# Matmul with batch normalisation: x and w loaded as bf16 by casting DMAs, and a streamed operand with a step of two

## The chip, the cores and the metric

One core of a Trainium2 chip. The metric is the device time of one execution in microseconds (us), the median of several. A profile shows one execution; its span is about 1.8 us shorter than the time. Runs are sorted into fast and slow by time and by the granted TensorE clock. The profile of the kernel before (span 296.1) fell on a run marked slow, a little above the median of its fast ones.

## The reference

```python
batch, m, k, n = 16, 512, 1024, 768
y = np.matmul(x, weight)                       # x: 16 x 512 x 1024, weight: 1024 x 768, fp32
mean = np.mean(y, axis=(0, 1), keepdims=True)  # per column, over all 8192 rows
var  = np.var(y, axis=(0, 1), keepdims=True)
out  = gamma * (y - mean) / np.sqrt(var + eps) + beta
```

The statistics of a column need all 8192 rows, so nothing can be stored before all of x has been multiplied by that column's weights.

## The kernel before

x comes in tiles of 256 rows (1 MB of fp32, `q` = 0 to 31). Each tile is brought in by four DMAs: quarter `i` of the columns goes to partitions 32i to 32i+31. GpSimd casts a tile to bf16, putting two rows side by side in a 4-byte word; VectorE transposes 32x32 blocks of such words; TensorE multiplies. A unit of work, called a *matmul tile* here, is 8 matmuls of 128x512: one of 6 column tiles (`nt`) times one of 16 chunks of 512 rows (`c`). Before the statistics of the first three column tiles (`GA = 3`) are complete, 63 of the 96 matmul tiles are done: all six column tiles for the first five chunks, three for the other eleven.

```python
def load_x(q):
    x_st = stage.tile([P, QT, KQ], f32, tag="st")          # three buffers
    rows = x_flat[q * QR:(q + 1) * QR].rearrange("(t r) k -> r t k", r=32)
    for i in range(4):
        eng = nc.sync if i < 2 else nc.scalar
        seq(eng.dma_start(x_st[32 * i:32 * i + 32], rows[:, :, KQ * i:KQ * (i + 1)]))

def cast_x(q, part):                                        # GpSimd, two parts of a tile
    x_bf = xbpool.tile([P, UP, KQ, 2], bf16, tag="xb")
    ...
def turn_x(q, part):                                        # VectorE
    ...
    seq(nc.vector.transpose(dst[:, half, part * UP:(part + 1) * UP], src))

def mm(nt, c):
    for jj in range(KT):
        seq(nc.tensor.matmul(y_ps, w_sb[:, jj, nt * P:(nt + 1) * P], xT[c][:, jj, :], ...))
def bn(nt, c):   seq(nc.vector.bn_stats(stats[:, nt, c, :], py[nt, c]))
def keep(nt, c): seq(nc.scalar.copy(y_sb, py.pop((nt, c))))
...
# all of these are put in order by a planned time: at(t, fn, ...)
at(t, load_affine)        # the 12 small gamma and beta DMAs, on GpSimd
```

The order on each engine is fixed by planned times, so a VectorE statistic can stand behind a transpose whose load is late.

## Time and profile before

| | before |
|---|---|
| time, median (range) | 296.28 us (295.21 to 297.46) |
| last transpose of x ends (the last load lands at 162.2) | 172.1 us |
| T1: statistics of the first three column tiles complete, aggregation starts | 193.3 us |
| T1 to the end | 102.8 us |
| mean rate over the span, HBM | 209 GB/s |

T1 is where the first bn aggregate starts in the chain of work. Everything before it is loading and multiplying; everything after is the output stage. The rows behind this table are in the prediction.

### The profile page before, as it was taken

How to read it: one execution, taken by the hardware profiler on the slowest of the kernel's cores; microseconds unless marked ns; L12 is line 12 of the kernel's file. 1: busy time of each engine (PE TensorE's matmuls, PEld its weight loads, DVE VectorE, ACT ScalarE, POOL GpSimd, SP SyncE). 2: the span in 40 equal slices, each digit the busy share in tenths (PEclk: the TensorE clock that was granted, in tenths of full speed). 3: DMA queues.
4: the chain of work that ended last, by engine and by line, in shares of the span. 5: the costliest groups of instructions: out<-in, count | busy, mean ns of one | idle time of the engine just before them, and what ended most of it. 6: DMA issues, size and time to landing. Idle time of an engine off the chain costs nothing.

```text
span 296.1 us, 3319 instructions
## 1 busy us (share of the span) xinstructions
PE 210.9 (71%) x1132; PEld 102.7 (35%) x1152; DVE 149.6 (51%) x285; ACT 99.4 (34%) x154; POOL 89.3 (30%) x83
## 2 busy tenths in 40 slices
PE   0019996597097875695647659989897999997630
PEld 0003442233043332232213224446564555554530
DVE  0344653626435554545452173387766656656751
ACT  2001221112122212121102033339796866566230
POOL 0333545436636565564642940000000000000000
PEclk9999999879779999797887959999999999999655
DMA  7999999999999999999999000007999797666997
GB/s 175 304 232 297 208 251 264 220 209 211 206 203 213 235 220 225 231 220 221 223 231 170 3 1 2 0 0 265 360 357 363 259 278 217 178 197 179 281 265 215
DMA packets 71889, 62.10 MB, mean 210 GB/s; under 512 B 3264, under 2 KB 71872, under 8 KB 71872
## 3 DMA queue, kind: packets, MB, share of 16 engines
q1 hardware_dynamic: 52448, 43.52, 57.3%
q10 hardware_dynamic: 19040, 18.35, 30.4%
q8 instruction: 9, 0.15, 0.2%
q0 software_dynamic: 384, 0.01, 0.1%
q14 instruction: 8, 0.07, 0.1%
HBM read 36.71 MB, written 25.17 MB: 209 GB/s over the span
## 4 chain that ended last, share of the span: by engine, by line
DMA 56%; PE 26%; DVE 6%; POOL 5%; ACT 4%; issue 2%; ACTq 0%; SPq 0%; DVEq 0%; POOLq 0%
DMA x_st<-in_x_dram 46%; PE y_ps L156 23%; DMA out_dram<-o_sb 8%; PE o_ps L193 3%; ACT o_sb L201 3%; POOL x_bf L136 3%; DMA w_st<-in_weight_dram 2%; DVE y_sb L180 2%; DVE stats L162 1%; POOL beta_sb L106 1%; POOL gamma_sb L105 1%; DVE o_sb L203 1%; ACT y_sb L167 1%; DVE mv L172 0%; DVE xT_sb L150 0%
## 5 line engine op out<-in xcount | busy, mean ns | idle before, releaser
L156 PE MATMUL y_ps<-xT_sb,w_sb 128*128 128x512 bf16 x748 | 187.9, 403 | 65.5 <-ACT y_sb L167 43.3
L156 PEld LDWEIGHTS <-w_sb 128*128 128x128 bf16 x768 | 77.6, 103 | 164.2 <-issue 82.5
L167 ACT CAST y_sb<-y_ps 128x512 bf16<-128x512 f32 x96 | 56.0, 588 | 163.4 <-DMA x_st<-in_x_dram 92.6
L136 POOL CAST x_bf<-x_st 128x1024 bf16<-128x1024 f32 x64 | 82.1, 1328 | 84.0 <-DMA x_st<-in_x_dram 81.8
L150 DVE STREAM_TRANSPOSE xT_sb<-x_bf 128x512 f32<-128x512 f32 x64 | 45.4, 711 | 82.0 <-POOL x_bf L136 82.0
L162 DVE BATCH_NORM_STATS2 stats<-y_ps 128x6 f32<-128x512 f32 x96 | 65.0, 678 | 36.5 <-PE y_ps L156 36.2
L201 ACT CAST o_sb<-o_ps 128x768 f32<-128x768 bf16 (+1 forms) x52 | 44.9, 886 | 24.5 <-DMA out_dram<-o_sb 13.0
L193 PE MATMUL o_ps<-ident,y_sb 128*128 128x128 bf16 x384 | 31.2, 231 | 9.8 <-DVE y_sb L180 6.9
L180 DVE TENSOR_SCALAR y_sb<-y_sb,scale,shift 128x512 bf16<-128x512 bf16 x96 | 33.2, 404 | 0.0
L193 PEld LDWEIGHTS <-y_sb 128*128 128x128 bf16 x384 | 26.2, 104 | 19.1 <-DVE y_sb L180 9.3
L122 DVE CAST w_sb<-w_st 128x2048 bf16<-128x2048 f32 x3 | 3.7, 1228 | 12.1 <-DMA w_st<-in_weight_dram 12.1
L203 DVE CAST o_sb<-o_ps 128x1024 f32<-128x1024 bf16 x4 | 4.9, 1225 | 6.1 <-DMA out_dram<-o_sb 5.2
L105 POOL DMA_DIRECT2D gamma_sb<-in_gamma_dram x6 | 3.4, 559 | 0.0
L106 POOL DMA_DIRECT2D beta_sb<-in_beta_dram x6 | 3.2, 536 | 0.0
L172 DVE BATCH_NORM_AGGREGATE mv<-stats 128x2 f32<-128x96 f32 x6 | 3.2, 561 | 0.0
L174 DVE RECIPROCAL scale<-std 128x1 f32<-128x1 f32 (+1 forms) x4 | 0.7, 167 | 3.9 <-ACT std L173 3.9
L97 ACT ACT_TABLE_LOAD x1 | 1.3, 1283 | 0.7 <-PEq L301 0.7
L173 ACT ACTIVATE std<-mv,eps_sb 128x1 f32<-128x1 f32 (+1 forms) x4 | 1.2, 304 | 0.8 <-DVE mv L172 0.8
L176 DVE TENSOR_TENSOR tmp<-mv,scale 128x1 f32<-128x1 f32 (+1 forms) x4 | 0.6, 160 | 0.1
L177 DVE TENSOR_TENSOR shift<-beta_sb,tmp 128x1 f32<-128x1 f32 (+1 forms) x4 | 0.6, 160 | 0.1
L175 DVE TENSOR_TENSOR scale<-scale,gamma_sb 128x1 f32<-128x1 f32 (+1 forms) x4 | 0.6, 159 | 0.1
masks.py:199 POOL TENSOR_SCALAR_AFFINE_SELECT ident<-ident 128x128 bf16<-128x128 bf16 x1 | 0.3, 288 | 0.0
(7 smaller groups left out, 0.9 us busy)
## 6 DMA issues: line engine op xcount, KB each, us to landing
x_st<-in_x_dram SPq DMA_DIRECT2D x64, 256.0 KB, 8.5
x_st<-in_x_dram ACTq DMA_DIRECT2D x64, 256.0 KB, 8.7
out_dram<-o_sb SPq DMA_DIRECT2D x16, 768.0 KB, 4.7
out_dram<-o_sb SPq DMA_DIRECT2D x24, 512.0 KB, 3.6
w_st<-in_weight_dram SPq DMA_DIRECT2D x6, 256.0 KB, 6.8
w_st<-in_weight_dram ACTq DMA_DIRECT2D x6, 256.0 KB, 6.7
gamma_sb<-in_gamma_dram POOLq DMA_DIRECT2D x6, 0.5 KB, 2.2
beta_sb<-in_beta_dram POOLq DMA_DIRECT2D x6, 0.5 KB, 2.3
```

What stands on the lines that cost most here:

```text
L105: seq(nc.gpsimd.dma_start(gamma_sb[:, nt:nt + 1], gamma[nt * P:(nt + 1) * P, None]))
L106: seq(nc.gpsimd.dma_start(beta_sb[:, nt:nt + 1], beta[nt * P:(nt + 1) * P, None]))
L122: seq(nc.vector.tensor_copy(w_sb[:, :, n0:n0 + WN], wst.pop(part)))
L136: seq(copy(x_bf.rearrange("p u k h -> p h u k"), xs[q].rearrange("p (h u) k -> p h u k", h=2)[:, :, part * UP:(part + 1) * UP, :],))
L150: seq(nc.vector.transpose(dst[:, half, part * UP:(part + 1) * UP], src))
L156: seq(nc.tensor.matmul(y_ps, w_sb[:, jj, nt * P:(nt + 1) * P], xT[c][:, jj, :], start=(jj == 0), stop=(jj == KT - 1),))
L162: seq(nc.vector.bn_stats(stats[:, nt, c, :], py[nt, c]))
L167: seq(nc.scalar.copy(y_sb, py.pop((nt, c))))
L180: seq(nc.vector.tensor_scalar(y[nt, c], y[nt, c], scale[:, nt:nt + 1], shift[:, nt:nt + 1], op0=ALU.mult, op1=ALU.add,))
L193: seq(nc.tensor.transpose(o_ps[:, s, a, :], cols, ident))
L201: seq(nc.scalar.copy(ost[key][:, part], src))
L203: seq(nc.vector.tensor_copy(ost[key][:, part], src))
```

## The change

x and w are brought in by GpSimd DMAs that cast on the way, so the GpSimd casts of x and the VectorE casts of w go, and half as many bytes reach SBUF. A 4-byte word then holds two neighbouring columns of one row, not two rows. After the transpose the even and the odd columns lie interleaved, so a matmul reads its streamed operand with a step of two, and w is laid out to match. Three smaller things go with it: four buffers for a tile of x in place of three, w in two parts in place of three, and the 12 gamma and beta DMAs now stand behind all loads on GpSimd. The diff is abridged.

```diff
+    XB = 4
-        x_st = stage.tile([P, QT, KQ], f32, tag="st")
+        x_bf = xbpool.tile([P, QT, KQ], bf16, tag="xb")
         rows = x_flat[q * QR:(q + 1) * QR].rearrange("(t r) k -> r t k", r=32)
         for i in range(4):
-            eng = nc.sync if i < 2 else nc.scalar
-            seq(eng.dma_start(x_st[32 * i:32 * i + 32], rows[:, :, KQ * i:KQ * (i + 1)]))
-    def cast_x(q, part): ...
+            seq(nc.gpsimd.dma_start(x_bf[32 * i:32 * i + 32], rows[:, :, KQ * i:KQ * (i + 1)]))
 ...
-            eng = nc.sync if i < 2 else nc.scalar
-            seq(eng.dma_start(w_st[32 * i:32 * i + 32], ...))
-    def cast_w(part): ...
+            for e in range(2):
+                seq(nc.gpsimd.dma_start(w_sb[32 * i:32 * i + 32, :, e, n0:n1], rows[i, e, :, :, n0:n1]))
 ...
-        for jj in range(KT):
-            seq(nc.tensor.matmul(y_ps, w_sb[:, jj, nt * P:(nt + 1) * P], xT[c][:, jj, :], ...))
+        for jw in range(JW):
+            for e in range(2):
+                seq(nc.tensor.matmul(y_ps, w_sb[:, jw, e, nt * P:(nt + 1) * P], xT[c][:, jw, :, e], ...))
 ...
-                cols = y[nt, c][:, half * QR:(half + 1) * QR].rearrange("p (m h) -> p h m", h=2)[:, h]
-                seq(nc.tensor.transpose(o_ps[:, s, a, :], cols, ident))
+                seq(nc.tensor.transpose(o_ps[:, s, a, :], y[nt, c][:, i * P:(i + 1) * P], ident))
```

## The prediction

> **What bounds the kernel now.** I read the page's chain of work first, then the chain in order of time, then the queue view in two narrow windows, then the costly groups.
>
> The chain that ended last, by line:
>
> ```profile
> DMA 56%; PE 26%; DVE 6%; POOL 5%; ACT 4%; issue 2%; ACTq 0%; SPq 0%; DVEq 0%; POOLq 0%
> DMA x_st<-in_x_dram 46%; PE y_ps L156 23%; DMA out_dram<-o_sb 8%; PE o_ps L193 3%; ACT o_sb L201 3%; POOL x_bf L136 3%; DMA w_st<-in_weight_dram 2%; DVE y_sb L180 2%; DVE stats L162 1%; POOL beta_sb L106 1%; POOL gamma_sb L105 1%; DVE o_sb
> ```
>
> Loading x alone is 46% of the span. The chain in order of time shows where that stretch ends (start, length, what):
>
> ```profile
> 158.16 4.03 DMA x_st<-in_x_dram
> ...
> 162.29 1.33 POOL x_bf L136
> 163.62 0.59 POOL gamma_sb L105
> ...
> 169.48 0.53 POOL beta_sb L106
> 170.00 1.34 POOL x_bf L136
> 171.36 0.71 DVE xT_sb L150
> ...
> 173.33 7.33 PE y_ps L156 x25
> 180.71 10.74 PE y_ps L156 x49
> ...
> 193.27 1.39 DVE mv L172 x3
> ```
>
> So there are three stages: loading, until the last transpose of x ends at 172.1 us; a remainder of matmuls (78 of them), until the statistics of the first three column tiles are complete at 193.3 (call this T1); and the output stage, from T1 to 296.1, which is 102.8 us. In the last, TensorE is busy nearly throughout until 272, and then stores drain. The 12 small gamma and beta DMAs put 6.4 us into the path between the last two casts.
>
> Why does loading take so long? 35.65 MB in some 160 us is 220 GB/s with the DMA engines never idle. Two windows of 1 us in the queue view, first at 12 us and then at 19 us:
>
> ```profile
> DMA packets 358, 0.35 MB, mean 345 GB/s; under 512 B 21, under 2 KB 358, under 8 KB 358
> ## 3 DMA queue, kind: packets, MB, share of 16 engines
> q10 hardware_dynamic: 181, 0.17, 56.0%
> q1 hardware_dynamic: 177, 0.17, 54.5%
> ```
>
> ```profile
> DMA packets 235, 0.23 MB, mean 229 GB/s; under 512 B 11, under 2 KB 235, under 8 KB 235
> ## 3 DMA queue, kind: packets, MB, share of 16 engines
> q10 hardware_dynamic: 200, 0.20, 97.6%
> q1 hardware_dynamic: 35, 0.03, 16.2%
> ```
>
> When both queues move equally, 345 GB/s; when one queue does nearly all, 229. SyncE's queue (q1) loads partitions 0 to 63, ScalarE's (q10) partitions 64 to 127, each DMA to 32 partitions. So I read the slow rate as the SBUF side: one half of the partitions takes about 220 GB/s.
>
> **What the Trainium skill says.**
> 1. "SBUF — State Buffer", section "Door 1: The DMA port swizzle": partitions 0 to 31, and 0 to 63, reach 8 of the 16 ports, 64 to 127 the other 8; the limit for eight ports is about 218 GB/s. The trace agrees (229 with a little from the other half, 345 with both).
> 2. "DMA: Bandwidth & Descriptors", section "SWDGE vs HWDGE vs iDMA": a DMA that casts must be issued by GpSimd, whose cores write the descriptors in software. In the trace a GpSimd DMA of 128 descriptors takes 0.53 us of the engine (the beta rows). Nothing in the trace shows one of 256.
> 3. "SBUF — State Buffer", the note on cachelines: lines of 16 bytes, two hits per line are enough for full speed. A step of two in bf16 makes four. The trace has a case on the weight side: y_sb is read with a step of two, w_sb densely, and the loads take 104 and 103 ns. For the streamed operand nothing shows it.
> 4. Same page, "Who interferes with whom": two-port VectorE copies hold GpSimd off from writing descriptors. The only such copies in the loading stage are the three casts of w, and they go.
>
> The groups that the change touches:
>
> ```profile
> L156 PE MATMUL y_ps<-xT_sb,w_sb 128*128 128x512 bf16 x748 | 187.9, 403 | 65.5 <-ACT y_sb L167 43.3
> L136 POOL CAST x_bf<-x_st 128x1024 bf16<-128x1024 f32 x64 | 82.1, 1328 | 84.0 <-DMA x_st<-in_x_dram 81.8
> L150 DVE STREAM_TRANSPOSE xT_sb<-x_bf 128x512 f32<-128x512 f32 x64 | 45.4, 711 | 82.0 <-POOL x_bf L136 82.0
> L162 DVE BATCH_NORM_STATS2 stats<-y_ps 128x6 f32<-128x512 f32 x96 | 65.0, 678 | 36.5 <-PE y_ps L156 36.2
> L106 POOL DMA_DIRECT2D beta_sb<-in_beta_dram x6 | 3.2, 536 | 0.0
> ```
>
> GpSimd, VectorE and TensorE all wait for the loads here, directly or by one step.
>
> **The change part by part.**
> - *Removed:* 64 casts on GpSimd (82.1 us) and 3 on VectorE (3.7 us). They lay beside the loads, save two casts' latency of 1.33 us per tile of x in how early a transpose and so a refill can start. ScalarE no longer issues loads, so its copies out of PSUM no longer queue behind a load's wait (TensorE lost 43.3 us to those copies). The gamma and beta DMAs now come after all loads on GpSimd: 6.4 us off the path.
> - *Moved:* the same 35.65 MB are read from HBM, but 128 + 16 DMAs now come from one GpSimd queue, and half the bytes are written into SBUF. In one queue the quarters of x come one after another, so mostly one half of the ports is in use. If that half takes 220 GB/s of bf16, it no longer limits: that would be 440 GB/s of fp32 read. I then take the best rate that loads of 1 KB pieces reach in this trace, 340 to 345 GB/s: 0.77 us per DMA of 256 KB, 3.1 us per MB.
> - *GpSimd's cost:* if 0.53 us were all per descriptor, 256 would take 1.06 us; if all fixed, 0.53. I take 0.7 to 0.8, so about level with the transfer. The program's order also shows eight completion semaphores in rotation: each DMA waits for the one eight before it, so 2 MB are in flight. At 340 GB/s that is 6.2 us, above the 2.2 us that a small GpSimd DMA takes to land, so the queue stays fed.
> - *Transposes:* 32 of 128x1024 words in place of 64 of 128x512. From 0.711 us for 512 and an estimated one word per cycle of 0.96 GHz (533 ns, so 178 fixed): 1.25 us each, 40 us in place of 45.4. No gain by itself.
> - *TensorE:* same 768 matmuls of 0.216 us (8 in 1.73 us in the chain); I assume that the step of two costs nothing.
>
> *The sum.* Start: 8 weight DMAs (1 MB), two tiles of x, then 2 MB of weights, 5 MB in all: at about 0.55 us each for the smaller ones and 0.75 for x, GpSimd has issued these by 16 us; the weights have landed at about 20. Then 30 tiles of x: 30 x 3.1 = 92 us, so the last lands at 112 and is transposed at 114. The order on VectorE fixes what follows: 15 statistics stand behind the last transpose (13 before). TensorE can be some 3 tiles ahead: before, 78 matmuls, or 9.75 tiles of 8, remained, and took 21.2 us. Now 11.75 remain: 20.3 us, plus about 1.7 for a cold start and the last statistics, so T1 = 136. The output stage has the same instructions in the same order on VectorE and SyncE: 102.8 us. End: 136 + 103 = 239; I say 240.
>
> The floor if loads were infinitely fast: TensorE has 63 tiles x 1.73 = 109 us before T1, two of them before 20 us: T1 = 20 + 105.5 + 1 = 126.5, end 229.
>
> **The rivals.**
> (a) *Descriptor writing becomes the bound.* At 1.0 us per DMA of x: 20 + 120 + 2 + 22 = 164, end 267. For it: GpSimd does all loads alone, and 0.53 us for 128 has an unknown split. Against: an instruction has a fixed part.
> (b) *The casting transfer is slow, or a single load queue is,* so that some 220 GB/s of fp32 stay the limit: 30 x 4.77 = 143, T1 = 187, end 290, nearly nothing gained but the gamma loads. For it: no single-queue load above 240 GB/s is in this trace. Against: a single queue stores at 360 GB/s (mean of 207 to 230 us), so an engine can do it.
> (c) *The step of two halves the matmul rate.* 768 x 0.43 = 330 us of matmuls: far slower, near 400. For it: nothing measured on the streamed side. Against: the weight side shows no cost.
> (d) *Loads are faster than 345 GB/s:* then TensorE bounds, 229 to 233.
>
> **Range and chances.** I weigh the main case and (d) at 55%, (a) or something halfway to it at 27%, (b) at 11%, (c) or another loss at 7%. The range 228 to 280 holds the main case and most of (a). Faster by over 2% means under 290.2: 0.87; within 2%: 0.06; slower: 0.07.
>
> **What would show it.** Right: the load rate near 340 GB/s until about 112 us, GpSimd's DMA instructions at 0.7 to 0.8 us, transposes at 1.25 us, matmul spacing 0.216 us, T1 near 136, and 103 us from there to the end. (a) shows as GpSimd issuing back to back at about 1 us with idle DMA engines; (b) as DMA engines fully busy at 220 GB/s; (c) as 8 matmuls in well over 1.73 us in the output stage. What makes it wrong most likely is the load rate, to which the end follows one for one: each 0.1 us per DMA of x is 12 us.

## The result, and the profile after

| | before | after | predicted |
|---|---|---|---|
| time, median (range) | 296.28 (295.21 to 297.46) | 243.24 (242.32 to 244.05) | 240 |
| last transpose of x ends | 172.1 | 109.0 | 114 |
| first matmul | 20.9 | 17.2 | two tiles before 20 |
| T1 | 193.3 | 134.8 | 136 |
| T1 to the end of the span | 102.8 | 106.8 | 103 |

The ratio is 0.821 (95% interval 0.817 to 0.825). A ratio is the mean time of one kernel's fast runs over that of the other's fast runs of the same rounds, so it is not quite the ratio of the medians quoted. All four runs of the kernel before on this chip count as fast, at 295 to 297 us. On two other chips, where its fast runs were at 289 to 293, the same step gave 0.835 (0.830 to 0.840, run c1) and, with an order that changed nothing, 0.837 (0.827 to 0.847, run e6). So the gain is 16 to 18%.

The chain of work that ended last, by engine and by line, for the kernel after:

```profile
PE 70%; DMA 15%; ACT 5%; DVE 4%; POOL 2%; issue 2%; ACTq 0%; POOLq 0%; DVEq 0%
```

The DMA's 56% have become 15%, most of it the stores at the end; TensorE's 26% have become 70%. In order of time (start, length, what), the whole loading stage is now one row of matmuls:

```profile
12.34 4.85 DMA w_sb<-in_weight_dram
17.19 11.40 PE y_ps L138 x40
...
29.23 1.24 DVE xT_sb L131
...
30.52 103.54 PE y_ps L138 x456
...
134.08 0.70 DVE stats L144
134.78 1.39 DVE mv L154 x3
```

456 matmuls in 103.54 us are 0.227 us each, where the prediction counted 0.216. The wait before 17.19 is put down to a weight load, but the second transpose of x also ends only at 17.1 (it starts at 15.89 and takes 1.25), so the start waits for both. VectorE's own order after the last transpose (start, length, engine, and in brackets the idle time before) shows the same from the other side:

```profile
107.76 1.25 DVE L131 STREAM_TRANSPOSE xT_sb<-x_bf 128x1024 f32<-128x1024 f32 x1 [0.18 <-DMA gamma_sb<-in_gamma_dram]
108.93 0.66 DVE L144 BATCH_NORM_STATS2 stats<-y_ps 128x6 f32<-128x512 f32 x1
110.51 0.70 DVE L144 BATCH_NORM_STATS2 stats<-y_ps 128x6 f32<-128x512 f32 x1 [0.92 <-PE y_ps L138]
112.33 0.70 DVE L144 BATCH_NORM_STATS2 stats<-y_ps 128x6 f32<-128x512 f32 x1 [1.11 <-PE y_ps L138]
```

From 110 us on every statistic waits for its matmuls, 1.81 us apart, and 14 of them follow. The groups of the changed lines (busy us, mean ns, then idle before):

```profile
L138 PE MATMUL y_ps<-xT_sb,w_sb 128*128 128x512 bf16 x768 | 182.2, 393 | 17.3 <-DMA w_sb<-in_weight_dram 17.2
...
L120 POOL DMA_DIRECT2D x_bf<-in_x_dram x128 | 73.1, 576 | 17.9 <-issue 6.6 <-DMA x_bf<-in_x_dram 4.6 <-DVE stats L144 2.5
...
L131 DVE STREAM_TRANSPOSE xT_sb<-x_bf 128x1024 f32<-128x1024 f32 x32 | 39.4, 1231 | 17.0 <-DMA x_bf<-in_x_dram 16.8
...
L111 POOL DMA_DIRECT2D w_sb<-in_weight_dram x16 | 8.8, 554 | 1.9 <-DMA x_bf<-in_x_dram 0.8
```

GpSimd spends 0.576 us on a DMA of 256 pieces, and 0.542 us (median) on one of 128 pieces: nearly all of it is fixed. The idle time before these matmuls fell from 65.5 to 17.3 us, 17.2 of it before the first one. (A piece is an unbroken run of the source in the program, 1 KB for x; the number of descriptors is not in the trace.) In the queue view of the kernel after, 17 of the 40 slices of the window 30 to 110 us read 190 to 194 GB/s, at a mean of 174; DMA bytes are counted as written here, at half size, so 193 is 386 GB/s of fp32 read: the steady best, and not the mean. Over the stage, 120 DMAs were issued from 16.7 to 103.1 us, 0.72 us each.

In the output stage one group of 8 matmuls took 3.28 us, and the granted clock there was half (two rows of the chain, then the window with its clock in the third place from the end):

```profile
172.02 3.28 PE y_ps L138 x8
...
176.11 1.80 PE y_ps L138 x8
172.00:175.40 3.40, 3.40 (x12) 1.30 (x10) 1.84 (x7) 1.29 (x2) 0.00 (x0) 0.51 0.69 249
```

### The profile page after: what moved, and what is told of

Its sections match the earlier page's. It is cut to its first block, busy times and chain, and to the rows that moved or that the text cites. A ratio compares the mean times of both kernels' runs of the same rounds, so it can differ in the third digit from the quotient of the medians.

```text
span 241.6 us, 3150 instructions
## 1 busy us (share of the span) xinstructions
PE 204.7 (85%) x1152; PEld 98.9 (41%) x1152; DVE 143.6 (59%) x250; ACT 100.1 (41%) x154; POOL 89.2 (37%) x163
## 4 chain that ended last, share of the span: by engine, by line
PE 70%; DMA 15%; ACT 5%; DVE 4%; POOL 2%; issue 2%; ACTq 0%; POOLq 0%; DVEq 0%
PE y_ps L138 65%; DMA out_dram<-o_sb 11%; PE o_ps L173 4%; ACT o_sb L181 4%; POOL w_sb L111 2%; DMA w_sb<-in_weight_dram 2%; DMA x_bf<-in_x_dram 2%; DVE y_sb L162 1%; DVE stats L144 1%; DVE mv L154 1%; ACT y_sb L149 1%; DVE xT_sb L131 1%; DVE o_sb L183 1%; ACT std L155 0%; DVE scale L156 0%
## 5 line engine op out<-in xcount | busy, mean ns | idle before, releaser
L138 PE MATMUL y_ps<-xT_sb,w_sb 128*128 128x512 bf16 x768 | 182.2, 393 | 17.3 <-DMA w_sb<-in_weight_dram 17.2
L138 PEld LDWEIGHTS <-w_sb 128*128 128x128 bf16 x768 | 73.4, 97 | 113.2 <-issue 12.2
L144 DVE BATCH_NORM_STATS2 stats<-y_ps 128x6 f32<-128x512 f32 x96 | 66.8, 696 | 64.6 <-PE y_ps L138 64.6
L120 POOL DMA_DIRECT2D x_bf<-in_x_dram x128 | 73.1, 576 | 17.9 <-issue 6.6
L131 DVE STREAM_TRANSPOSE xT_sb<-x_bf 128x1024 f32<-128x1024 f32 x32 | 39.4, 1231 | 17.0 <-DMA x_bf<-in_x_dram 16.8
L111 POOL DMA_DIRECT2D w_sb<-in_weight_dram x16 | 8.8, 554 | 1.9 <-DMA x_bf<-in_x_dram 0.8
```

The costliest lines, as they stand in the source:

```text
L111: seq(nc.gpsimd.dma_start(w_sb[32 * i:32 * i + 32, :, e, n0:n1], rows[i, e, :, :, n0:n1],))
L120: seq(nc.gpsimd.dma_start(x_bf[32 * i:32 * i + 32], rows[:, :, KQ * i:KQ * (i + 1)]))
L131: seq(nc.vector.transpose(dst[:, half], src))
L138: seq(nc.tensor.matmul(y_ps, w_sb[:, jw, e, nt * P:(nt + 1) * P], xT[c][:, jw, :, e], start=(jw == 0 and e == 0), stop=(jw == JW - 1 and e ...
```

## The experiments

The theory after the result: the loads of the kernel before were held by the side of SBUF that they write, because each DMA goes to partitions of one half (0 to 63 or 64 to 127); halving the bytes lifts that limit; then TensorE sets the pace, slowed a little by the step of two. The rivals: the gain came from leaving the two hardware queues (with ScalarE's issue standing between its copies) or from dropping the casts; the longer spacing of matmuls came from TensorE running without gaps; the loads still set the pace. A further one, the fourth buffer of x, falls with e2, which has four buffers too.

Runs e1, e2, e3, e5 and e7 give wrong results.

### e2: the same DMAs without the cast

```diff
-        x_bf = xbpool.tile([P, QT, KQ], bf16, tag="xb")
+        x_bf = stage.tile([P, QT, KQ], f32, tag="st")            # STAGE = 4
-        src = xs.pop(q).rearrange("p t k -> p (t k)").bitcast(f32)
+        src = xs.pop(q).rearrange("p t k -> p (t k)")[:, :QT * KQ // 2]
-                    ... xT[c][:, jw, :, e],
+                    ... xT[c][:, jw, :, 1],
```

The transposes and matmuls are as many and as large as in the changed kernel. Only the loads of x write 256 KB in place of 128 KB.

> The changed kernel with x brought in as fp32 by the same GpSimd DMAs, no cast, full-size writes (wrong result: the upper halves are multiplied for even and odd columns alike). If halving the bytes written to one half of the ports is what made loading fast: about 220 to 230 GB/s of x, 1.14 to 1.2 us per DMA, the last x landing near 160 us, T1 near 183 us and the end near 290 us. If the gain came from leaving the SyncE and ScalarE queues and dropping the GpSimd casts: 0.72 us per DMA as in the changed kernel and 243 us.

Measured: 303.79 us median (301.08 to 308.08), T1 at 200.2. The window 40 to 90 us of its queue view:

```profile
DMA packets 3124, 10.25 MB, mean 205 GB/s; under 512 B 626, under 2 KB 626, under 8 KB 3122
```

The whole gain is gone, although all other parts of the change are in place. The rival of the queues and the casts falls. The rate was lower than I had expected (205, not 220 to 230) because the 229 of the kernel before had some traffic to the other half in it: from 60 to 61 us, where q10 moved 10 of 212 packets, that kernel reads 203. And e2 is slower than the kernel before, whose two queues overlapped for part of the time (222 GB/s from 30 to 160 us).

### e3: full-size writes, but across all partitions

```diff
 # on top of e2
-        rows = x_flat[q * QR:(q + 1) * QR].rearrange("(t r) k -> r t k", r=32)
+        rows = x_flat[q * QR:(q + 1) * QR].rearrange("(t r) k -> r t k", r=P)
-            seq(nc.gpsimd.dma_start(x_bf[32 * i:32 * i + 32], rows[:, :, KQ * i:KQ * (i + 1)]))
+            seq(nc.gpsimd.dma_start(x_bf[:, 2 * i:2 * i + 2], rows[:, :, KQ * i:KQ * (i + 1)]))
```

> As e2_fp32_32, but each of the four DMAs of a tile spans 128 partitions with the same 256 pieces of 1 KB (wrong result: rows lie where columns should). If it is the half of the ports that limits full-size writes: 340 GB/s or more, at most 0.77 us per DMA, T1 at 135 to 140 us, end 243 to 248 us. If it is the bytes written as such, or the single queue: as slow as e2_fp32_32, near 290 us.

Measured: 242.57 us (241.53 to 242.82), T1 at 138.2. The same window:

```profile
DMA packets 5124, 16.82 MB, mean 336 GB/s; under 512 B 1024, under 2 KB 1024, under 8 KB 5121
```

Same bytes, same queue, no cast, and packets of 4 KB in both runs (the queue view has the pieces of 1 KB put together): 336 GB/s in place of 205. So it is not the number of bytes written that counts but how many partitions share them. One thing else differs in e3, and in e5 below: a DMA reads its rows in another order, and no run changes that order alone. In e3 GpSimd needs 0.714 us per DMA and is the pace of the loads.

### e5: the kernel before, with loads across all partitions

```diff
-        rows = x_flat[q * QR:(q + 1) * QR].rearrange("(t r) k -> r t k", r=32)
+        rows = x_flat[q * QR:(q + 1) * QR].rearrange("(t r) k -> r t k", r=P)
-            seq(eng.dma_start(x_st[32 * i:32 * i + 32], rows[:, :, KQ * i:KQ * (i + 1)]))
+            seq(eng.dma_start(x_st[:, 2 * i:2 * i + 2], rows[:, :, KQ * i:KQ * (i + 1)]))
```

> The kernel before, only each load of x spanning 128 partitions (wrong result). If half of the ports limits its loads: x at 340 GB/s or more, the last transpose near 115 us, T1 near 137 us, end near 240 us, with the GpSimd casts still in place. If the alternation of the two queues or the casts are the limit: 296 us unchanged.

Measured: 248.16 us (246.18 to 248.75), T1 at 143.9. The window 40 to 90 us:

```profile
DMA packets 17977, 17.39 MB, mean 348 GB/s; under 512 B 1057, under 2 KB 17971, under 8 KB 17971
## 3 DMA queue, kind: packets, MB, share of 16 engines
q1 hardware_dynamic: 8987, 8.67, 54.5%
q10 hardware_dynamic: 8984, 8.66, 53.7%
```

The kernel before, with its GpSimd casts and its two queues, comes within 5 us of the changed one as soon as its loads spread over all partitions. It is 8 us above what I expected: the last transpose ended at 124.5 us and not near 115, and VectorE waited 29.4 us for the GpSimd casts. This cannot be used as it stands: the quarters of the columns have to lie in different groups of 32 partitions for the block transpose, and these loads put them elsewhere.

### e8: the kernel before, each queue alternating between the halves

```diff
-        for i in range(4):
-            eng = nc.sync if i < 2 else nc.scalar
+        for i in (0, 3, 2, 1):
+            eng = nc.sync if i % 2 == 0 else nc.scalar
```

> The kernel before, each queue alternating between the halves of the partitions: SyncE loads quarters 0 and 2, ScalarE quarters 3 and 1 (correct). If the halves are the limit and each queue alone now reaches both: over 260 GB/s on average in the loading stage and 260 to 280 us. If one queue works one DMA at a time: the two queues can still meet in the same half, some 230 GB/s, 285 to 296 us.

Measured: 304.85 us (302.17 to 307.03), ratio 1.045 (1.034 to 1.057); correct. It is slower, and by more than the range of either branch. One microsecond of its queue view, at 60 us:

```profile
DMA packets 202, 0.20 MB, mean 204 GB/s; under 512 B 3, under 2 KB 202, under 8 KB 202
## 3 DMA queue, kind: packets, MB, share of 16 engines
q10 hardware_dynamic: 103, 0.10, 56.9%
q1 hardware_dynamic: 99, 0.10, 56.4%
```

Here both queues move equally and the rate is still 204. Equal queues alone are therefore not what makes loads fast. The profile doesn't list the partition of a packet, but the trace has each packet's queue, start and size, and a DMA of x is 256 packets. Counting them off in the order of issue puts SyncE on quarter 2 and ScalarE on quarter 3 in this microsecond: the same half. Over 5 to 160 us, half a microsecond after a slice of 0.1 us in which one half of the partitions got 90% of the bytes or more, the median rate was 202 GB/s (933 slices); after one in which both halves got about the same, it was 259 (179 slices). The rate 0.6 us later correlates with the balance of the halves at 0.64, and with the balance of the queues at 0.25. So e8 fits the halves; it lost because its queues met in one half most of the time.

The same question has to be put to the kernel before. In some of its microseconds the queues moved almost equally and slowly: from 16 to 17 us, 132 packets of q1 and 103 of q10, at 225 GB/s. In windows of 0.2 us, 16.0 to 16.2 and 16.8 to 17.0, they turn out to take turns:

```profile
q1 hardware_dynamic: 50, 0.05, 103.3%
q10 hardware_dynamic: 5, 0.01, 9.8%
...
q10 hardware_dynamic: 41, 0.04, 109.1%
q1 hardware_dynamic: 2, 0.00, 1.5%
```

Side by side for several microseconds they reached 335 GB/s (9 to 13 us) and 342 (22 to 26). From 30 to 160 us they mostly took turns, and the mean was 222. Why they fell into taking turns is open.

### e6 and e7: alternating the halves within GpSimd's single queue

```diff
 # e6: on the changed kernel; e7: on e2
-        for i in range(4):
+        for i in (0, 2, 1, 3):
```

> The changed kernel with the four DMAs of a tile of x in the order of quarters 0, 2, 1, 3, so that neighbours in the queue go to opposite halves of the ports (correct). If half of the ports still limits the casting loads (193 GB/s written against 206 in e2_fp32_32) and neighbours overlap: more than 193 GB/s written; the end gains at most 1 to 2 us, since TensorE sets most of the pace. If GpSimd's pace, buffers or the read side limit: unchanged, 243 us.

> e2_fp32_32 (full-size writes, wrong result) with the quarters in the order 0, 2, 1, 3. If it is the half of the ports and neighbours in one queue overlap: well over 206 GB/s and an end under 285 us. If the engines work one DMA at a time, so that the halves take turns anyway: 206 GB/s and 303 us unchanged.

Measured: e6 243.39 us (241.92 to 245.24), correct, unchanged, and its best slices read the same 190 to 194 GB/s. e7 288.68 us (286.58 to 290.93), 231 GB/s in the window where e2 had 205. So neighbours in one queue do overlap a little, which helps full-size writes by 13% in rate. That falls between my two branches. Casting loads get nothing from it; what holds them at 386 GB/s of fp32 stays open.

### e1: the step of two taken away

```diff
-                    ... xT[c][:, jw, :, e],
+                    ... xT[c].rearrange("p jw m e -> p (jw m e)")[:, (2 * jw + e) * CH:(2 * jw + e + 1) * CH],
```

> The changed kernel with the streamed operand read densely (wrong result: the words stay interleaved). If the step of two is what stretches a matmul from 0.216 to 0.227 us and TensorE sets the pace of the loading stage too: 8 matmuls back to 1.73 us, T1 (the first bn aggregate) at 134.8 - 63 x 8 x 0.0106 = 129.5 us, and the end 768 x 0.0106 = 8 us earlier, 235 us. If the longer spacing comes of TensorE running without gaps (power or clock), nothing changes: 1.81 us and 243 us. If the loads set the pace of the loading stage, T1 stays at 134.8 and only the output stage gains 3 us.

Measured: 236.41 us (235.41 to 238.24), T1 at 131.0. Two rows of its chain, one before T1 and one after:

```profile
118.99 10.74 PE y_ps L138 x49
...
140.77 1.73 PE y_ps L138 x8
```

Eight matmuls take 1.73 us again, where the kernel after has 1.81, at a granted clock of 1.00 in both. The step of two costs (1.81 - 1.73) / 8 = 0.010 us per matmul, about 8 us of TensorE's time over 768. T1 moved by 3.7 us and not by 5.3: between 102 and 109.5 us TensorE stood still three times in e1, 2.3 us in all, and before that the chain runs through the loads, while in the kernel after TensorE has no gap from 17.2 us until after T1. So TensorE set the pace before T1 in the changed kernel, but with little to spare over the loads.

The output stage got 103.9 us long, 3 us less, as expected, but not for that reason alone: e1 has no stretch of half clock there. All three traces of the changed kernel do (after, c1 and e6: 3.4 us near 172, one group of 8 matmuls at 2.95 to 3.28 us), and their output stages take 106.8 to 107.3. v1, v2 and v3 below have the step of two and no such stretch: 104.6, 104.6 and 105.1. So some 2 us go with the half clock and some 1 with the step (single executions, all fast); what halves the clock is open. And e2, e3 and e7, with the step of two and four staging buffers in place of three (the outputs use them too), take 102.5 each: there the step cannot be seen at all.

### e4: the gamma and beta DMAs out of the way, in the kernel before

```diff
-    at(t, load_affine)
+    at(t + 20.0, load_affine)
```

> The kernel before, with only the 12 gamma and beta DMAs put behind the last casts of x on GpSimd. If they stood in the path between the last two casts, as the prediction said: the last transpose and the end 6.4 us earlier, ratio about 0.978. If the last load is what the path waits for anyway: unchanged.

Measured: 288.46 us (286.77 to 293.1), ratio 0.987 (0.981 to 0.992). The means of the fast runs are 288.1 and 291.9, so 3.9 us and not 6.4 are gained. The interval of the ratio makes that 2.2 to 5.5 us. The claim was right in kind, and some 40% of the 6.4 us did not show. The trace of e4 suggests why: its last transpose ends at 165.3 us, 6.8 earlier than in the (slow) profile of the kernel before, but TensorE now runs without a gap from 154.1 until after T1, so T1 no longer waits for the last load.

### v1, v2, v3: an earlier start, correct versions

With TensorE setting the pace, its start at 17.2 us is worth attacking. v1 brings all of w in as fp32 over SyncE, beside the loads of x, with casts on ScalarE. v2 adds 130 small transposes on TensorE before the first matmul. v3 brings only the first 256 columns of w in that way, over SyncE and ScalarE, and leaves the rest to GpSimd (its diff is abridged). The unedited changed kernel ran beside v1 and v2 as c1.

```diff
 # v3
+        if part == 0:
+            w_st = xtpool.tile([P, JW, 2, n1], f32, tag="xT")
         for i in range(4):
             for e in range(2):
+                if part == 0:
+                    eng = nc.sync if i < 2 else nc.scalar
+                    seq(eng.dma_start(w_st[32 * i:32 * i + 32, :, e, :], rows[i, e, :, :, :n1]))
+                else: ...                                # GpSimd, as in the changed kernel
+    def cast_w(part): seq(nc.scalar.copy(w_sb[:, :, :, n0:n1], wst.pop(part)))
```

> The changed kernel itself, unedited, as the yardstick for the runs beside it: 243 us, a chain of 70% TensorE.

> A correct version: x as in the changed kernel, but the weights come in as fp32 over the SyncE queue beside it and ScalarE casts them, so GpSimd starts on x at once. If TensorE's late start (17.2 us) and its own pace set T1: first matmul near 12 us, T1 near 130 us, end near 238 us. If the loads of x set T1, it gains about as much, since x starts 4.8 us earlier and has no weights between its tiles. If the full-size weight writes crowd the ports: x later, no gain.

> v1_w_early with 130 small transposes of the identity on TensorE before the first matmul. If the first matmuls are slow because the engine was idle before (285 ns each for the first 40 in the changed kernel against 227 later): some 2 us off, 236 us. If the slow first matmuls come of waits for weights: no difference from v1_w_early.

> The changed kernel with only the first 256 columns of the weights brought in as fp32 over SyncE and ScalarE and cast by ScalarE, all else as it is (correct). In v1_w_early 3 MB of full-size weight writes crowded the first tiles of x; here it is 1 MB. If that was the reason: first matmul near 13 us in place of 17.3, T1 near 131 us, end near 239 us. If even 1 MB crowds x, or if x sets T1: 243 us.

| | time, median (range) | ratio to before (95%) | first matmul of y | T1 |
|---|---|---|---|---|
| c1, the changed kernel | 244.03 (242.08 to 245.06) | 0.835 (0.830 to 0.840) | 17.3 | 134.8 |
| v1, all of w over SyncE | 243.57 (243.07 to 245.23) | 0.835 (0.831 to 0.839) | 19.2 | 138.9 |
| v2, and a warm TensorE | 245.02 (243.68 to 246.20) | 0.839 (0.833 to 0.845) | 20.6 | 139.4 |
| v3, 256 columns of w over both | 238.60 (238.06 to 239.21) | 0.820 (0.815 to 0.825) | 14.5 | 132.3 |

v1 missed: the second tile of x was transposed only from 17.9 us, 2 us later than in the changed kernel, although GpSimd began on x at 1.4 us. It was the third branch of what I had written: the weights, 3 MB at full size, crowd the first tiles of x. Its T1 is 4 us later than that of c1, and its end is not, because its output stage has no stretch of half clock. v2 missed too. Its small transposes ended at 12 us, and the second tile of x was transposed only at 20.6; in the windows 15 to 20 and 20 to 30 us its granted clock was 0.70 and 0.81 (c1: 1.00 in both), so whatever the small transposes had done was lost by then. It says nothing about what a well-placed one would gain. v3 has 1 MB of full-size weights at the start:

```profile
10.54 1.25 DVE L142 STREAM_TRANSPOSE xT_sb<-x_bf 128x1024 f32<-128x1024 f32 x1 [10.54 <-DMA x_bf<-in_x_dram]
13.23 1.25 DVE L142 STREAM_TRANSPOSE xT_sb<-x_bf 128x1024 f32<-128x1024 f32 x1 [1.45 <-DMA x_bf<-in_x_dram]
```

Its first tile is transposed 2.3 us earlier than in the kernel after (12.83 there), and its first matmul and its T1 are earlier by about as much (2.7 and 2.5 us). Beside e6, which differs from the changed kernel only in an order that changed nothing, it is 4.8 us or 2.0% faster, and it is correct: the best version. The other 2 us come after T1, where its trace has no stretch of half clock and that of e6 has one; whether the earlier start has to do with that is not shown.

## Why the prediction was right, point by point

- **What bounds the loads: right, and shown.** The reading of the two windows (one half of the partitions takes about 220 GB/s) carried the forecast. e2, e3 and e5 confirm it, and e8 fits it. The number was nearer 205 than 220. The two windows alone did not prove it: others, such as 16 to 17 us, have nearly equal queues at 225 GB/s, and only finer windows show them taking turns (see e8).
- **Two readings of the trace: wrong, without effect.** x and w are 36.7 MB and not 35.65 (18.35 MB in each queue's loads), so the mean was nearer 230 GB/s. And the "128 descriptors" of a beta DMA are its elements: the queue view has 384 packets for the 12 small DMAs, 32 each.
- **GpSimd's cost: too high.** I took 0.7 to 0.8 us per DMA of x; it is 0.576. Doubling the pieces from 128 to 256 adds 0.034 us, so rival (a), at 1.0 us, was far off.
- **The load rate: too low.** I took 340 to 345 GB/s of fp32, the best rate in the trace before. It was 386 at its steady best and 0.72 us per DMA on average against 0.77, so the last transpose ended at 109.0 and not at 114.
- **Transposes: right,** 1.23 us against 1.25.
- **The step of two: wrong.** "I assume that the step of two costs nothing": e1 shows 0.010 us per matmul, 5%. The weight side, on which I had argued, does not show it.
- **T1: right by errors that offset.** The loads were 5 us faster, but 25.8 us and not 22 followed the last transpose, since TensorE was behind: 14 matmul tiles at 1.81 us make 25.4. So that 240 came so near was in part luck. Taken as a story, rival (d) came true, with its floor raised: 126.5 us plus 63 x 0.08 us for the step is 131.5, and the first 40 matmuls, at 0.285 us each in place of 0.227, add 2.3 of the rest to 134.8. Why they are slow is not shown. The main case, in which the loads set the end one for one, did not hold; e1 shows that it was close.
- **The output stage: 106.8 us against 102.8.** Of the 4 us, some 2 go with the 3.4 us of half clock near 172 (v1 to v3, without it, take 104.6 to 105.1), and about 1 with the step of two (e1). The rest is not settled.
- **Rivals (b) and (c):** a single casting queue is not slow, and the step of two does not halve the rate.

The term for gamma and beta, 6.4 us in the prediction, is 3.9 us by e4.

## What to carry to other kernels

Before blaming DMA bandwidth, compare a stretch in which the queues move side by side with one in which they take turns, in windows short enough to tell these apart, and ask which partitions each of them writes; then spread or halve what goes to one half. When a wait as large as that for the loads goes, compute the pace of the next engine with its new operand pattern, not with the old one: here TensorE took over, 5% slower than its old spacing. Two errors that offset each other make a right total; only the times at the stage borders showed which step had failed.

## What the Trainium skill lacked or had wrong

- "SBUF — State Buffer", section "Can I just issue two DMAs to hit both halves?", says no, with a gain of 6%. In the kernel before, two queues with one half each moved 335 and 342 GB/s while they ran side by side (9 to 13 and 22 to 26 us), against 205 for loads to one half at a time in one queue (e2). Over 30 to 160 us, where they mostly took turns, it was 222, 8% more, which is near the page's figure. Within one queue, alternating the halves gave 231 (e7), 13% more.
- "SBUF — State Buffer", the note on cachelines, has two hits per 16-byte line suffice for full speed. A streamed bf16 operand with a step of two, four hits per line, took 0.227 us per matmul against 0.216 dense (kernel after and e1).
- "DMA: Bandwidth & Descriptors" gives no rate for a DMA that casts. fp32 to bf16, in pieces of 1 KB to 32 partitions each: 386 GB/s read at the steady best.
- The same page, section "Anatomy of one DMA — SWDGE (gpsimd) path", calls the time of descriptor generation small and variable, with no number. On GpSimd it was 0.542 us for 128 pieces, 0.576 for 256 on 32 partitions (kernel after), and 0.714 for 256 on 128 partitions (e3), which there set the pace of the loads.
